# Seams and down part of an MLP laid out anew: early places, a fixed product order, four X banks, some pairs stored in two parts

## The chip, the cores and the metric

The kernel runs on one core of a Trainium2 chip. The metric is the device time of one execution, in microseconds. The profile comes from one further execution with the hardware profiler on. Engines are named as in the profile: PE (TensorE, matmuls), PEld (its weight loads), DVE (VectorE), ACT (ScalarE), POOL (GpSimd) and SP (SyncE, whose queue issues nearly all transfers).

## What is computed

One layer of a decoder trunk, in float32, for 2048 tokens of width 1024:

```python
a   = rmsnorm(x, norm_pre_mix)
mix = token_mixer(a, ...)                  # mLSTM heads and latent attention heads, then @ w_out
x   = x + rmsnorm(mix, norm_post_mix)
m   = rmsnorm(x, norm_pre_mlp)
y   = jnp.square(jax.nn.relu(m @ w_up)) @ w_down      # D_FF = 4096
x   = x + rmsnorm(y, norm_post_mlp)
```

Only the end of the token mixer (the product with w_out) and the MLP matter here.

## The kernel before

**Precision.** Each float32 factor of a product is split into a high part, which is a cast to fp32r on ACT, and a low part, which is a subtraction on DVE. A product is three matmuls: high by high, high by low, low by high. So every operand that reaches PE costs one cast and one subtraction first.

**Fewer products.** Both MLP products work on 2 x 2 blocks with seven products instead of eight (Winograd's form). The operands of the seven are the blocks themselves or sums of them, called s1 to s4 for the weights, and "T" factors for the activations. The seven results are combined through three chains of PSUM banks, X, Y and Z: products 0, 4, 5 and 6 go one after the other into one X bank, 1 and 3 into a Y bank, 2 into a Z bank (`CHAINS`). Between two products into the same bank the running sum is read out, and the next product waits for that read-out: product 3 waits for the first read-out of Y, 4 for the first of X, 5 for the second, 6 for the third.

**Output projection** (`group`, `matrix`, `transposes`). Eight groups of 256 tokens are multiplied by w_out, which lies split in SBUF. Each token tile is then normalised, the residual is added (`post`), and the result x1 is stored in DRAM (x1d). After every 512 tokens (a row block, `blk`) eight groups of four PE transposes turn x1 around (L1822) into one of two PSUM banks, ACT scales them by the gain (L1827) into one of two staging tiles `xg`, and they are stored as raw blocks in DRAM (`xd`).

**Factors of the up part.** `sums_of_rows` (L1856 on) loads four raw blocks, makes four sums on DVE (L1867) and stores these (L1870). `factor` (L1887 on) loads one of the seven factors, for each of four slices kk of 128 columns, and splits it on ACT and DVE (L1899, L1903). The tiles of factors 0 to 3 lie in a pool of their own, those of 4 to 6 in a pool that opens when the whole output projection is over (`open_b`).

**Up part** (`up`). 32 units: two halves g of the tokens by 16 pairs p of 256 hidden columns. A unit is seven products of 12 matmuls of 512 columns. `first_factors` loads its weights into two row buffers (`wr`), makes the four sums (L1959) and splits seven factors (L1989, L1992) into the 12 weight places of the ring `w`. The results are squared after a relu on ACT (L2063, L2066), summed on DVE (L2097) into the seven hidden factors and stored in DRAM (`hd`, L2111).

**Down part** (`down`, `hidden`). Eight chunks c of two pairs each, by eight units u of 256 tokens; a unit is seven products of six matmuls (L2209 to L2211). For each unit and each of the two pairs the seven hidden factors are loaded as one tile of 128 x 896 (L2179) and split (L2183, L2187). The weights of a chunk are 14 tiles out of 20 places, 8 of them in a pool `w2` that opens after the up part. The places are given out alternating between the two pairs (`2 * j + e`). Results are added to the accumulators y in SBUF, mostly on DVE (L2230), two per unit in the middle chunks by way of ACT and GpSimd (L2243, L2246). In the last chunk `finish` normalises each row tile: squares on ACT (L2279), a total on DVE (L2282), a root on GpSimd (L2285), the scaling with the gain on DVE (L2288), and the residual on GpSimd or, for tiles 11 and 15, on DVE (L2291); then the store (L2294).

**What sets the order.** All work after the first stages is declared as operations of a planner, `Plan`: engine, cost in ns, the operations that it comes after, a key, and the buffers ("rings") that it takes and frees. `Plan.run` simulates the engines: at each step it takes the operation that can start first, and among equal starts the one with the lowest key. The code is emitted in that order, and `pin` fixes the resulting order on PE, ACT, DVE and POOL. So each engine works through a list that is settled when the kernel is built, and an instruction that waits holds up everything behind it on its engine. `"X"` operations open and close pools and take no time. A pool that opens in memory or banks of a closed one waits for that one's last readers.

Of the kernel before, what the change touches and what calls it, by code (L numbers as in the profile page):

```python
# [185 lines left out]
def trunk(ctx: ExitStack, tc: tile.TileContext, x, xT, pos, wu, uqw, ukw, uvw, wout, wup, wdn, cols, rows, consts, edge, out, dbg=None):  # L186
# [38 lines left out]
    maskb = top.tile([P, P], BF16, tag="maskb", name="maskb")  # L225
    identb = top.tile([P, P], BF16, tag="identb", name="identb")
# [84 lines left out]
    def masks():  # L311
        act.copy(maskb, maskT)
        act.copy(identb, ident)
        act.copy(identr, ident)
# [794 lines left out]
    a2 = a1 = av = ar2 = pq = pS = po = trig = V = maskneg = None  # L1109
# [39 lines left out]
    def switch3():  # L1149

        nonlocal av, ar2, pS, po, V
        s_b.close()
        av = sb(pa, "av", 1, "right")
        ar2 = sb(pa, "ar2", 2, "right")
# [478 lines left out]
    for name, bufs in (("w", WB), ("wx", 4), ("wr", 2), ("xr", XR), ("st", ST), ("hr", 3), ("rb", 2), ("accA", 2), *((f"h{k}", 1) for k in range(KD))):  # L1633
        pl.ring(name, bufs)

    def wtile(name, ring="w"):

        return (pools["o1"] if ring == "wx" else pools["w2"] if ring == "w2" else pools["work"]).tile(
            [P, 2, TB], F32R, tag=ring, name=name, bufs=dict(w=WB, wx=4, w2=W2B)[ring]
        )  # L1640
# [11 lines left out]
    def right():  # L1652
        pa.close()
        pools["xa"] = sb(ctx, "xa", 1, "right")
        pools["o3"] = sb(po2, "o3", 1, "right")
        pools["pmB"] = pp(po2, "pmB", 1, "right")
        pools["ptr"] = pp(po2, "ptr", 2, "right")
# [8 lines left out]
    for name, bufs in (("accB", 1), ("ptr", 2), ("xt", 2), ("xg", 2), ("x1", XB)):  # L1666
        pl.ring(name, bufs)
# [3 lines left out]
    def matrix(k):  # L1671
        t = {}
        ring = "w" if 2 * k < WB else "wx"
# [5 lines left out]
        def hi(c):  # L1679
            wo[k, c] = wtile(f"wo{k}_{c}", ring)  # L1680
            act.copy(wo[k, c][:, 0], t["r"][:, c * TB : (c + 1) * TB])
# [6 lines left out]
        for c in range(2):  # L1688
            b = pl.op("Activation", 520, lambda c=c: hi(c), [a], key, take=(ring,))
            o_w[k, c] = pl.op("DVE", 602, lambda c=c: lo(c), [b], key, free=[("wr", a)])  # L1690
            w_free[k, c] = (ring, b)

    o_x1, x1s = {}, {}

    def group(g):
# [50 lines left out]
        for k in range(KD):  # L1746
            c, d = tile_(k)
            for t in range(GT):
# [5 lines left out]
                if k == 0:  # L1754
                    o_acc.append(prev[t])

        def post(t):
# [42 lines left out]
            pl.op("SP", 500, store, [f], key, free=[("x1", e)], kb=512)  # L1800
# [11 lines left out]
    def transposes(blk):  # L1812
        g, s = divmod(blk, 2)

        def one(k):
            q = {}
            i = (7 if s else 0) if k < 4 else (3 if s else 2)

            def tr():
                q["p"] = pools["ptr"].tile([P, 4, P], F32, tag="t", name=f"xtr{blk}_{k}")  # L1820
                for t in range(4):
                    pe.transpose(q["p"][:, t], x1s[4 * blk + t][:, k * P : (k + 1) * P], ident)  # L1822
                q["p"] = q["p"].rearrange("p t i -> p (t i)")

            def raw():
                q["x"] = pools["o3"].tile([P, TB], F32, tag="xg", name=f"xg{blk}_{k}", bufs=2)
                act.activation(q["x"], q["p"], AF.Copy, scale=pools["gcol"][:, k : k + 1])  # L1827
# [3 lines left out]

            key = END + 20 * (TB // n) * (blk + 1) + 2
            a = pl.op("PE", 4 * 110, tr, [o_x1[4 * blk + t][1] for t in range(4)], key, take=("ptr",), free=[("x1", o_x1[4 * blk + t][0]) for t in range(4)])
            b = pl.op("Activation", 571, raw, [a], key, take=("xg",), free=[("ptr", a)])
            o_xd[g, i, k % 4] = pl.op("SP", 500, store, [b], key, free=[("xg", b)], kb=256)

        for k in range(KD):
            one(k)
# [14 lines left out]

    def sums_of_rows(g, kk):

        t = {}  # L1856
        key = UP + (g - 1) * 80 + 2 * kk + 5 if g == 0 else UP + 40 + 20 * kk
# [14 lines left out]
        p = pl.op("X", 0, place, [o_xd[g, i, kk] for i in (0, 7, 3, 2)], key, take=("xr",) * 4)  # L1872
        a = {i: pl.op("SP", 500, lambda i=i: load(i), [p, o_xd[g, i, kk]], key, kb=256) for i in (0, 7, 3, 2)}
        t1 = pl.op("DVE", 602, lambda: sub(0, 7, 0), [a[0], a[7]], key)
        t3 = pl.op("DVE", 602, lambda: sub(7, 3, 7), [a[3], t1], key)
        t2 = pl.op("DVE", 602, lambda: sub(3, 3, 0), [t3], key)
        t4 = pl.op("DVE", 602, lambda: sub(2, 2, 3), [a[2], t2], key)
        for i, at, o in ((1, 0, t1), (5, 7, t3), (4, 3, t2), (6, 2, t4)):
            o_xd[g, i, kk] = pl.op("SP", 500, lambda i=i, at=at: store(i, at), [o], key, free=[("xr", p)], kb=256)
# [7 lines left out]
    def factor(g, i, kk):  # L1887
# [3 lines left out]
        pool_ = "xa" if i < 4 else "xb"  # L1891
# [14 lines left out]
        opened = o_right if i < 4 else o_open  # L1906
        last = [o_xo[0, i, kk][2]] if g else []
        a = pl.op("SP", 500, load, [o_xd[g, i, kk], opened] + (o_last_w[0, NP - 1] if g else []), key - 4, take=("xr",), kb=256)
        b = pl.op("Activation", 520, hi, [a, opened], key, take=(f"x{i}{kk}h",))
        c = pl.op("DVE", 602, lo, [b], key, take=(f"x{i}{kk}l",), free=[("xr", a)])  # L1910
# [3 lines left out]
    def open_a():  # L1914
        pA.close()
        pools["u0"] = pp(ctx, "u0", 1)

    o_openA = pl.op("X", 0, open_a, o_accA, UP)

    def open_b():  # L1920
        po1.close()
        po2.close()
        pools["u1"] = pp(ctx, "u1", 1, "right")
        pools["xb"] = sb(pX, "xb", 1, "right")
        pools["ub"] = sb(pB, "ub", 1)

    o_open = pl.op("X", 0, open_b, pl.groups["out"] + [o_openA], UP)
    for s in range(2):
        for z, bufs in (("X", 2), ("Y", 1), ("Z", 1)):
            pl.ring(f"{z}{s}", bufs, o_open if s else o_openA)  # L1930
    SLOTS = {"11": 2, "12": 1, "22": 1, "21": 1, "s1": 1, "s2": 1, "s4": 1, "p1": 1, "p5": 1, "u2": 1}
    for z, bufs in SLOTS.items():
        pl.ring(f"t{z}", bufs, o_open)
# [3 lines left out]

    def bank(s, z, name):
        return pools[f"u{s}"].tile([P, TB], F32, tag=z, name=name, bufs=2 if z == "X" else 1)

    def first_factors(nm, key, src, kind, ring, after=()):
# [22 lines left out]
        if up:  # L1964
            s1 = pl.op("DVE", 602, lambda: add("s1", (1, 0), (1, 1), add_), [a[1]], key - 10, take=("st",))
            s3 = pl.op("DVE", 602, lambda: add((1, 0), (0, 0), (1, 0), sub_), [s1, a[0]], key - 9)
            s2 = pl.op("DVE", 602, lambda: add("s2", "s1", (0, 0), sub_), [s1, a[0]], key - 9, take=("st",))
            s4 = pl.op("DVE", 602, lambda: add("s4", (0, 1), "s2", sub_), [s2], key - 8, take=("st",))
            what = [((0, 0), a[0]), ("s1", s1), ((0, 1), a[0]), ("s4", s4), ("s2", s2), ((1, 0), s3), ((1, 1), a[1])]
        else:  # L1970
            s1 = pl.op("DVE", 602, lambda: add("s1", (0, 1), (0, 0), sub_), [a[0]], key - 10, take=("st",))
            s3 = pl.op("DVE", 602, lambda: add((0, 1), (1, 1), (0, 1), sub_), [s1, a[1]], key - 9)
            s2 = pl.op("DVE", 602, lambda: add("s2", (1, 1), "s1", sub_), [s1, a[1]], key - 9, take=("st",))
            s4 = pl.op("DVE", 602, lambda: add("s4", (1, 0), "s2", sub_), [s2], key - 8, take=("st",))
# [6 lines left out]
        def one(i, w, o):  # L1981
# [12 lines left out]
            b = pl.op("Activation", 520, hi, [o], key - 8 + i, take=(ring[i],))  # L1994
            c = pl.op("DVE", 602, lo, [b], key - 8 + i, free=[("st", held[w])] if isinstance(w, str) else [("wr", p)])
# [7 lines left out]
    hd = {(p, g): dram.tile([4, P, 7, P], F32, tag=f"hd{p}_{g}", name=f"hd{p}_{g}") for p in range(NP) for g in range(2)}  # L2003
# [4 lines left out]
    def products(nm, s, i, pieces, passes, t, after, key, free, ns):  # L2008
# [4 lines left out]
        for j, piece in enumerate(pieces):  # L2013
# [6 lines left out]
            last = pl.op("PE", ns, mm, after[j] + ([last] if j else []) + after["all"], key, take=(f"{z}{s}",) if new and j == 0 else (), free=free[j])  # L2020
# [6 lines left out]
    def up(g, p):  # L2027
        nu = g * NP + p
        s = nu % 2
        key = UP + UNIT * nu  # L2030
        w = first_factors(f"u{g}_{p}", key, lambda e: wup[2 * p + e], "up", ["w"] * 7, [o_w[KD - 1, 1]])
# [4 lines left out]
        def product(i, after):  # L2036
# [12 lines left out]
            last = products(nm, s, i, [(kk,) for kk in range(4)], passes, t, af, key + 2.5 * i, fr, 660)  # L2049
# [18 lines left out]
        def both(o, after, free=()):  # L2068
            k = key + 10
            a = after if o != "21" else None  # L2070
            r = pl.op("Activation", 540, lambda: relu(o), [after], k, take=("t21",) if o == "21" else (), free=free)
            q = pl.op("Activation", 540, lambda: square(o), [r], k)
            return (r if o == "21" else a), q

        p1 = product(0, [o_openA])
        v1 = pl.op("Activation", 540, lambda: save("p1", "X"), [p1], key + 2, take=("tp1",))
        p5 = product(1, [])
        v5 = pl.op("Activation", 540, lambda: save("p5", "Y"), [p5], key + 2, take=("tp5",))
        p2 = product(2, [])
        c11 = pl.op("DVE", 640, lambda: plus("11", "Z", "p1"), [p2, v1], key + 5, take=("t11",), free=[(f"Z{s}", t_o(t, "Z", pl)), ("tp1", v1)])  # L2080
        p3 = product(3, [v5])
        p6 = product(4, [v1])
        v2 = pl.op("Activation", 540, lambda: save("u2", "X"), [p6], key + 8, take=("tu2",))
# [324 lines left out]
```

## Time and profile before

| | |
|---|---|
| median of 3 runs | 2621.9 us (2618.11 to 2624.91) |
| profiled execution | 2622.13 us |
| its span, first to last instruction | 2620.4 us |
| granted PE clock, mean | 0.982 |
| PE / DVE / ACT / POOL busy, share of the span | 95% / 72% / 50% / 32% |
| first up matmul starts at | 1277.3 us of the span |
| first down matmul starts at | 1932.96 us of the span |

A line of a timeline gives the start in the span, the duration, engine, line, operation, output and inputs, and in brackets how long the engine sat idle before it and what released it. A matmul's duration is longer than the distance to the next one's start, since matmuls are pipelined; how fast PE works is read from starts or from counts. A row of a table of stretches gives the stretch, its length, then for PE, PEld, DVE, ACT and POOL the busy time and the count of instructions, then the granted PE clock, the DMA share and GB/s. A line of a group gives count, busy time and mean duration, then the idle time before these instructions.

### The profile page before, as it was taken

To read this page: it belongs to the slowest core of one execution; us is meant where nothing else is said; L and a number is where in the kernel's file an instruction comes from. 1 tells how busy PE (TensorE), PEld (TensorE's weight loads), DVE (VectorE), ACT (ScalarE), POOL (GpSimd) and SP (SyncE) were. 2 spreads that over 40 slices of the span, in tenths; PEclk is the share of its full clock that TensorE was granted. 3 is DMA by queue.
4 is the path that set the end of the run, shared out by engine and by line. 5 is a ranking of instruction groups with operands and counts; after the bars stand their busy time and mean duration, and the time that the engine had idled before them with its cause. 6 is when DMAs were issued, how large, how long until landed. Compare 5 with 4: busy or idle time off the path is not lost. (4 is left out here: it accounts for less than half of the span.)

```text
span 2620.4 us, 33126 instructions
## 1 busy us (share of the span) xinstructions
PE 2486.6 (95%) x11107; PEld 1956.8 (75%) x11107; DVE 1895.7 (72%) x3090; ACT 1316.6 (50%) x2481; POOL 832.5 (32%) x673
## 2 busy tenths in 40 slices
PE   8999999899999999899899999999989999999997
PEld 6778787676677777687778888888867777787775
DVE  5876658699999999755676567656556677776788
ACT  5544444366666676544455556555544333433343
POOL 3442423367877787422000000000000222322235
PEclk9999999899999999999899999999989999999999
DMA  6555544400000000577886547645453333333346
GB/s 215 152 167 155 162 143 130 126 9 9 13 7 11 11 9 16 156 222 246 305 257 197 145 139 223 177 144 154 145 163 117 108 116 111 115 117 106 117 161 231
DMA packets 256179, 347.66 MB, mean 133 GB/s; under 512 B 28316, under 2 KB 169128, under 8 KB 255816
## 3 DMA queue, kind: packets, MB, share of 16 engines
q1 hardware_dynamic: 252424, 338.16, 42.3%
q0 software_dynamic: 3584, 7.39, 1.1%
q8 instruction: 87, 1.43, 0.2%
q14 instruction: 84, 0.69, 0.1%
HBM read 237.25 MB, written 108.22 MB: 132 GB/s over the span
## 5 line engine op out<-in xcount | busy, mean ns | idle before, releaser
L1467 POOL TENSOR_TENSOR pl<-p,ph 128x512 fp32r<-128x512 f32 (+1 forms) x267 | 336.2, 1273 | 144.2 <-ACT p L1463 90.7
L2246 POOL TENSOR_TENSOR y<-vd_0X,y 128x512 f32<-128x512 f32 x6 | 9.2, 1532 | 784.5 <-ACT vd_0X L2243 784.5
L1459 ACT ACTIVATE ph<-S 128x512 fp32r<-128x512 f32 (+1 forms) x320 | 170.7, 535 | 134.8 <-PE S L196 37.1
L1492 DVE SCALAR_TENSOR_TENSOR t<-ph,V,t 128x512 f32<-128x512 f32 x152 | 174.0, 1145 | 2.9
L194 PE MATMUL mm<-xh,wh 128*128 128x512 f32 x384 | 159.7, 416 | 9.5 <-ACT xh L339 7.9
L2187 DVE TENSOR_TENSOR hl<-hr,hh 128x896 fp32r<-128x896 f32 x128 | 147.0, 1154 | 18.6 <-ACT hh L2183 18.6
L196 PE MATMUL mm<-xh,wl 128*128 128x512 f32 x384 | 152.7, 398 | 0.0
L195 PE MATMUL mm<-xl,wh 128*128 128x512 f32 x384 | 152.4, 397 | 0.0
L1463 ACT ACTIVATE p<-S 128x512 f32<-128x512 f32 (+1 forms) x267 | 144.1, 541 | 9.7 <-POOL pl L1467 8.7
L1401 DVE TENSOR_REDUCE mp<-m 128x1 f32<-128x512 f32 x192 | 127.4, 681 | 21.3 <-PE m L1396 19.8
L2183 ACT CAST hh<-hr 128x896 fp32r<-128x896 f32 x128 | 115.8, 943 | 37.6 <-issue 8.5
L194 PE MATMUL S<-Qh,Kh 97*128 97x512 f32 (+1 forms) x320 | 123.0, 385 | 3.2 <-ACT p L1463 1.6
L1396 PE MATMUL m<-Kh,Qh 96*128 96x512 f32 (+2 forms) x320 | 113.0, 399 | 13.6 <-DVE mp L1401 10.3
L1479 PE MATMUL o<-pl,V 128*128 128x512 f32 (+1 forms) x320 | 121.0, 381 | 4.9 <-DVE pl L1467 2.6
L1476 PE MATMUL o<-ph,V 128*128 128x512 f32 (+1 forms) x320 | 120.5, 377 | 0.6 <-DVE ot L1547 0.5
L195 PE MATMUL S<-Ql,Kh 97*128 97x512 f32 (+1 forms) x320 | 119.5, 373 | 0.0
L196 PE MATMUL S<-Qh,Kl 97*128 97x512 f32 (+1 forms) x320 | 119.2, 372 | 0.0
L373 ACT CAST wh<-wr 128x1024 fp32r<-128x1024 f32 (+1 forms) x65 | 66.7, 1032 | 93.2 <-PE mm L195 56.4
L2063 ACT ACTIVATE t<-t 128x512 f32<-128x512 f32 x96 | 60.8, 633 | 95.5 <-DVE t L2058 94.4
L194 PE MATMUL op<-wo,hh 128*128 128x512 f32 x256 | 102.2, 399 | 2.3 <-DVE osm L1768 2.3
L195 PE MATMUL op<-wo,hh 128*128 128x512 f32 x256 | 100.7, 393 | 2.0 <-DVE wo L1684 2.0
L196 PE MATMUL op<-wo,hl 128*128 128x512 f32 x256 | 100.5, 393 | 0.0
(6388 smaller groups left out, 7658.2 us busy)
## 6 DMA issues: line engine op xcount, KB each, us to landing
hr<-hd SPq DMA_DIRECT2D x128, 448.0 KB
hd<-t SPq DMA_DIRECT2D x128, 256.0 KB
wr<-in_wu_dram SPq DMA_DIRECT2D x63, 512.0 KB
hd<-ts SPq DMA_DIRECT2D x96, 256.0 KB
xt<-in_x_dram SPq DMA_DIRECT2D x28, 512.0 KB
xf<-xd SPq DMA_DIRECT2D x56, 256.0 KB
hr<-hT SPq DMA_DIRECT2D x64, 128.0 KB
x1d<-x SPq DMA_DIRECT2D x16, 512.0 KB
```

The costliest lines, as they stand in the source:

```text
L194: pe.matmul(o, ah, bh, start=start, stop=False)
L195: pe.matmul(o, ah, bl, start=False, stop=False)
L196: pe.matmul(o, al, bh, start=False, stop=stop)
L1401: vec.tensor_reduce(mp["t"][:, j, kb : kb + 1], ps, axis=AX.X, op=ALU.max)
L1459: act.activation(t["h"][:, :w], t["S"][:, :w], AF.Exp)
L1463: act.activation(t["p"][:, :w], t["S"][:, :w], AF.Exp)
L1467: (pool if by_pool else vec).tensor_tensor(t["l"][:, :w], t["p"][:, :w], f32(t["h"][:, :w]), ALU.subtract)
L1476: pe.matmul(oo, v[:, 2:130], t["h"][:, :w], start=start, stop=False)
L1479: pe.matmul(oo, v[:, 2:130], t["l"][:, :w], start=False, stop=stop)
L1492: vec.scalar_tensor_tensor(to, hv, v0, acc["t"][:, TB - w :], ALU.mult, ALU.add)
L2183: act.copy(t["h"], t["r"])
L2187: vec.tensor_tensor(t["l"], t["r"], f32(t["h"]), ALU.subtract)
```

## The change

All of it is in the planner's declarations; the arithmetic of the products stays.

1. **Costs.** The planner's costs of the output projection and the MLP are set anew (casts 520 to 610, subtractions 602 to 690, three matmuls 660 to 695, read-outs 540 or 640 to 610 or 690).
2. **First seam.** Row blocks 2 and 3 are no longer transposed in the output projection. They are loaded again from x1d within the up part (keys from unit 3 on), four loads of 64 KB for each group of four transposes, which use the X banks and are scaled in place of the loaded tile. For the first half, factors 0, 1, 2 and 3 are split straight from the tiles of `sums_of_rows`, without the way through DRAM. The keys of the sums move earlier for the first half and later for the second.
3. **Banks and pools.** The two transpose banks become X0 and X1 of the up part; four X banks, two Y and two Z banks are separate rings. Y, Z and the working tiles `ub` open once the accumulators of the projection's first pool are read and its last matmul is done; X2 and X3 still open with `open_b`. Three slices of factor 4 move to `ub`. The slot of tile 11 goes from two buffers to one.
4. **Pairs in two parts.** Pairs 2, 6, 10 and 13 (`TWO`) are split into high and low part in the up part, through two tiles `hs`, and stored as 14 tiles; the down part loads both parts directly, with no cast and no subtraction.
5. **Down part.** Every weight place is a ring of its own. The places follow the order in which the last up units free them (`WORDER`), pair by pair (`7 * e + j`). The hidden tiles of the first two units of the first chunk take places of up factors 0, 1 and 2; all others are split in two pieces of 4 and 3 factors. The order of products on PE is written out: unit u's products 0 and 1, then 5 of the unit before, 2, 3, 6 of the unit before, 4. The last up unit's relu, squares and sums get an earlier key.
6. **Finish.** The gain is multiplied first (GpSimd; DVE for tiles 11 and 15), the scaling and the residual follow in one DVE instruction.
7. Two mask copies move from the start to the attention part (`switch3`).

```diff
-        if (g + 1) * n % TB == 0:
+        if (g + 1) * n % TB == 0 and (g + 1) * n <= HB:
             transposes((g + 1) * n // TB - 1)
...
+            if g:
+                key = UP + UNIT * (3 + 4 * s + k / 2)
+                r = pl.op("SP", 2000, load, [o_x1d[4 * blk + t] for t in range(4)] + [o_xo[0, 6, kk][1] for kk in range(4)], key - 10, take=("xr",), kb=256)
+                a = pl.op("PE", 4 * 110, tr, [r], key, take=(f"X{k % 4}",))
+                b = pl.op("Activation", 610, raw, [a], key, free=[(f"X{k % 4}", a)])
+                o_xd[g, i, k % 4] = pl.op("SP", 500, store, [b], key, free=[("xr", r)], kb=256)
+                return
...
-        for i, at, o in ((1, 0, t1), (5, 7, t3), (4, 3, t2), (6, 2, t4)):
-            o_xd[g, i, kk] = pl.op("SP", 500, lambda i=i, at=at: store(i, at), [o], key, free=[("xr", p)], kb=256)
+        def parts(i, o, n):
+
+            if g == 0:
+                at[i] = factor(g, i, kk, lambda: t[n], o, p)
+                return at[i]
+            return o
...
     def open_a():
         pA.close()
+        po1.close()
         pools["u0"] = pp(ctx, "u0", 1)
+        pools["ub"] = sb(pB, "ub", 1)
...
-    SLOTS = {"11": 2, "12": 1, "22": 1, "21": 1, "s1": 1, "s2": 1, "s4": 1, "p1": 1, "p5": 1, "u2": 1}
+    SLOTS = {"11": 1, "12": 1, "22": 1, "21": 1, "s1": 1, "s2": 1, "s4": 1, "p1": 1, "p5": 1, "u2": 1}
...
+    TWO = {p: p in (2, 6, 10, 13) for p in range(NP)}
+    hd = {(p, g): dram.tile([4, P, 14 if TWO[p] else 7, P], F32, tag=f"hd{p}_{g}", name=f"hd{p}_{g}") for p in range(NP) for g in range(2)}
...
+                b = pl.op("Activation", 610, hi, [made, *readers], k + 1, take=("hs",))
+                made = pl.op("DVE", 690, lo, [b], k + 1)
...
-        key = DN + 9.2 * (8 * c + u) + 2 * e
+        key = DN + 9.7 * (8 * c + u) + 2 * e
+        first = c == 0 and u < 2
+        parts = [(0, 4), (4, 3)]
+        if first:
+            tags = {(z, m): early[12 * u + 6 * e + 2 * n + m] for n, z in enumerate("rhl") for m in range(2)}
...
-            ring = ["w" if (14 * c + 2 * j + e) % (WB + W2B) < WB else "w2" for j in range(7)]
+            ring = [f"w{WORDER[(14 * c + 7 * e + j) % (WB + W2B)]}" for j in range(7)]
...
+    for u in range(NU + 1):
+        line += [(u, 0), (u, 1), (u - 1, 5), (u, 2), (u, 3), (u - 1, 6), (u, 4)]
+    line = [turn[x] for x in line if x in turn]
+    for a, b in zip(line, line[1:]):
+        pl.ops[b[0]][3].append(a[1])
```

More of the change, by code (lines that the diff above doesn't have):

```diff
@@ L1672, in matrix @@
         t = {}
-        ring = "w" if 2 * k < WB else "wx"
+        ring = ["wx" if 2 * k >= WB else f"w{2 * k + c}" for c in range(2)]
         def load():
@@ L2018, in mm @@
                 passes(t[z], *piece, new and j == 0, j == len(pieces) - 1)
-            last = pl.op("PE", ns, mm, after[j] + ([last] if j else []) + after["all"], key, take=(f"{z}{s}",) if new and j == 0 else (), free=free[j])
+            last = pl.op("PE", ns, mm, after[j] + ([last] if j else []) + after["all"], key, take=(bk(s, z),) if new and j == 0 else (), free=free[j])
             if new and j == 0:
@@ L2121, in trunk @@
         sums_of_rows(0, kk)
-    for i in range(7):
+    for i in range(4, 7):
         for kk in range(4):
@@ L2189, in hidden @@
-        a = pl.op("SP", 500, load, [o_dr, *o_hd[p, g]], key - 10, take=("hr2",), kb=448)
-        b = pl.op("Activation", 880, hi, [a], key - 5, take=("hh2",))
-        d = pl.op("DVE", 1003, lo, [b], key - 5, take=("hl2",), free=[("hr2", a)])
-        return t, d, [("hh2", b), ("hl2", d)]
+        key = DN + 9.7 * (8 * c + u) + 2 * e
[3 more added lines that the diff above has]
+            tags = {(z, m): early[12 * u + 6 * e + 2 * n + m] for n, z in enumerate("rhl") for m in range(2)}
+        else:
+            tags = {(z, m): f"{z}{e}{m}" for z in "hl" for m in range(2)}
@@ new lines, in new, with load @@
+        def new(z, m, dt):
+            if first:
+                t[z, m] = pools["xa"].tile([P, TB], dt, tag=tags[z, m], name=f"h{z}{m}_{c}_{u}_{e}")
+            else:
+                t[z, m] = pools["dr"].tile([P, parts[m][1] * P], dt, tag=tags[z, m], name=f"h{z}{m}_{c}_{u}_{e}", bufs=HHB)
+        def load(z, m, off):
+            j0, nj = parts[m]
+            new(z, m, F32 if z == "r" else F32R)
+            o = t[z, m][:, : nj * P]
+            dma(o if z == "r" else f32(o), hd[p, g][i][:, off + j0 : off + j0 + nj].rearrange("p j t -> p (j t)"))
@@ new lines, in loadr, with hi, lo @@
+        def loadr():
+            r = pools["dr"].tile([P, 7 * P], F32, tag="hr2", name=f"hr_{c}_{u}_{e}", bufs=HRB)
+            dma(r, hd[p, g][i].rearrange("p j t -> p (j t)"))
+            for m, (j0, nj) in enumerate(parts):
+                t["r", m] = r[:, j0 * P : (j0 + nj) * P]
+        def hi(m):
+            new("h", m, F32R)
+            w = parts[m][1] * P
+            act.copy(t["h", m][:, :w], t["r", m][:, :w])
+        def lo(m):
+            new("l", m, F32R)
+            w = parts[m][1] * P
+            vec.tensor_tensor(t["l", m][:, :w], t["r", m][:, :w], f32(t["h", m][:, :w]), ALU.subtract)
```

309 lines of the change are left out of this document (181 added, 128 removed).

## The prediction

> **What bounds the kernel now.** I read the page first, then a table of busy time by stage, then TensorE's own order of time at the three kinds of place where that table shows less work than time. The page says that TensorE is nearly always busy:
>
> ```profile
> span 2620.4 us, 33126 instructions
> ...
> PE 2486.6 (95%) x11107; PEld 1956.8 (75%) x11107; DVE 1895.7 (72%) x3090; ACT 1316.6 (50%) x2481; POOL 832.5 (32%) x673
> ```
>
> The product work is not touched by the change, so what it can gain is TensorE's lost time after the attention part. The stages: end of the output projection, its seam with the up part, the up part, its seam with the down part, seven chunks of the down part, the eighth, the tail. The x behind PE busy counts matmuls.
>
> ```profile
> core 0: us, PE busy (x) PEld busy (x) DVE busy (x) ACT busy (x) POOL busy (x), PEclk, DMA share, GB/s
> 1255.00:1277.30 22.30, 22.30 (x101) 18.31 (x100) 16.20 (x23) 11.66 (x23) 1.27 (x2) 1.00 0.94 334
> 1277.30:1304.10 26.80, 20.30 (x79) 15.23 (x78) 15.55 (x23) 13.98 (x25) 1.72 (x2) 0.75 0.77 254
> 1304.10:1915.00 610.90, 610.09 (x2618) 491.29 (x2617) 389.83 (x615) 340.87 (x600) 0.00 (x0) 1.00 0.60 178
> 1915.00:1933.00 18.00, 6.79 (x28) 4.58 (x26) 9.51 (x17) 8.67 (x14) 0.00 (x0) 0.78 0.60 191
> 1933.00:2520.00 587.00, 568.25 (x2362) 446.04 (x2363) 405.27 (x526) 222.19 (x338) 135.39 (x96) 0.99 0.37 114
> 2520.00:2610.00 90.00, 80.78 (x328) 59.70 (x326) 84.98 (x120) 35.27 (x76) 53.12 (x43) 1.00 0.69 230
> 2610.00:2620.40 10.40, 0.00 (x0) 0.00 (x0) 6.28 (x10) 1.44 (x4) 0.55 (x1) 0.73 0.50 176
> ```
>
> The up part is full: 610.9 / 2618 = 0.2333 us per 512-column matmul, my yardstick. A product of an up unit (12 matmuls) then takes 2.8 us, one of a down unit (6) 1.4 us, a down unit (7 products) 9.8 us. By this yardstick the second seam loses 18.0 - 28 x 0.2333 = 11.5 us, the seven chunks 587.0 - 2362 x 0.2333 = 35.9, the eighth 90.0 - 328 x 0.2333 = 13.5. In the first seam 32 of the 79 are short transposes:
>
> ```profile
> 1290.78 0.60 PE L1822 MATMUL xtr<-cst,x 128*128 128x128 f32 x4
> ...
> 1295.57 1.11 PE L1822 MATMUL xtr<-cst,x 128*128 128x128 f32 x4 [2.49 <-ACT xg L1827]
> ```
> ```profile
> 1294.83 0.69 ACT L1827 ACTIVATE xg<-xtr,gcol 128x512 f32<-128x512 f32 x1 [2.46 <-DMA xd<-xg]
> ```
>
> Four without a wait take 0.60 at most, say 0.45 by their starts (an estimate), so eight fours are 3.6 us, 47 products 11.0, and 26.8 - 14.6 = 12.2 us is lost. The rows tell by what: transposes of the last row block wait for ScalarE's scaling, and that for the store of a staging tile of which there are two. In all 12.2 + 11.5 + 35.9 + 13.5 = 73.1 us lost, and 10.4 of tail.
>
> **The first seam.** Blocks 2 and 3 leave the output projection. The up part opens all Y and Z banks and its working tiles once the last projection matmul is done and its pair of accumulators read, instead of (second set of banks, working tiles) after the whole post-processing; it takes its first two X banks from the earlier transposes, and gets factors 0 to 3 straight from the sums in SBUF: 16 loads and 4 stores of 256 KB fewer. So neither wait shown above is left. The 12 factor loads that remain now wait until all four sums have their staging tiles; behind them on SP stand weight loads, a unit ahead of need. New lateness can come from factors 5 and 6, whose tiles still open when all of the projection's post-processing is over; they are used 14 us into unit 0, and the planner can put products of unit 1 before them. I leave 2 us (bounds 0 and 6): 10.2 gained.
>
> The 16 fours that are moved cost 16 x 0.45 = 7 us of TensorE in the up part and free as much before it, where the row 1255 to 1277 has TensorE busy throughout: zero. Each also brings four load issues on SP, one ScalarE scaling and one store into the up part. They come due from unit 3 on, long after unit 0 frees the staging tiles, so loads lie ahead of need; were they not, TensorE's queue would stand behind each.
>
> **Pairs in two parts.** Pairs 2, 6, 10 and 13 are split after the activation: 4 pairs x 2 halves x 7 tiles = 56 casts on ScalarE, 56 subtractions on VectorE, 56 more stores. The price of each is in the rows of the same forms:
>
> ```profile
> L1899 ACT CAST x_01h<-xf x2: 603/612/621, 1155.5 to 1585.3; 128x512 fp32r<-128x512 f32 x2
> L1903 DVE TENSOR_TENSOR x_01l<-xf,x_01h x2: 683/688/693, 1156.2 to 1588.7; 128x512 fp32r<-128x512 f32 x2
> ```
> ```profile
> hd<-t SPq DMA_DIRECT2D x128, 256.0 KB
> ```
> ```profile
> L2187 DVE TENSOR_TENSOR hl<-hr,hh 128x896 fp32r<-128x896 f32 x113 | 125.0, 1109 | 14.6 <-ACT hh L2183 14.6
> ```
> ```profile
> L2183 ACT CAST hh<-hr 128x896 fp32r<-128x896 f32 x112 | 101.2, 944 | 16.3 <-issue 8.5 <-PE d_1X L2210 4.1 <-PE d_0X L2210 2.2
> ```
>
> That is 56 x 0.612 = 34 us of ScalarE and 56 x 0.688 = 39 of VectorE beside an up part in which they are busy 341 and 390 of 611: both have cover. In the down part 4 x 8 = 32 splits go, 32 x 1.109 = 35 us of VectorE and 30 of ScalarE. The other 96 are cut into pieces of 512 and 384 columns, 0.69 + 0.55 (in proportion between the two rows, an estimate) against 1.109: 96 x 0.13 = 12 us come back. VectorE nets 23 less of 490. For the denser up part I charge 2 us (bounds 0 and 10: one 1.2 us wait per two-part unit).
>
> **The second seam.** Now the first hidden tiles are loaded only when every store of the last up unit is issued:
>
> ```profile
> 1924.53 0.69 DVE L2097 TENSOR_TENSOR ts<-t,ts 128x512 f32<-128x512 f32 x1 [1.06 <-ACT t L2066]
> ```
> ```profile
> 1926.84 1.87 SPq L2179 DMA_DIRECT2D hr<-hd  x2
> ```
> ```profile
> 1931.97 1.99 ACT L2183 CAST hh<-hr 128x896 fp32r<-128x896 f32 x2 [3.75 <-DMA hr<-hd]
> ```
> ```profile
> 1932.96 0.79 PE L2209 MATMUL d_0X<-d,hh 128*128 128x512 f32 x1 [9.75 <-ACT hh L2183]
> ```
>
> From issue to use is 5.1 us, and the splits follow. The change puts the tiles of the first two down units into places of factors 0 to 2, free once product 2 of the last up unit is over, four products (11.2 us) before its end. 5.1 + 0.6 + 0.7 fits. The third unit's tiles still wait for the last store, but are due only 12 products, 16.8 us, into the down part. VectorE was idle 8.5 of the 18 us and gets 4 splits (5 us) more there, and some weights earlier. I leave 4 us (bounds 0 and 9): 7.5 gained. The slot of up tile 11, now one buffer instead of two, can be judged here: the products of a unit end at 1932.96 - 9.75 = 1923.2, its last store is issued before 1926.84, 3.6 us later (two-part pairs: 1.3 more), and the next unit writes the slot 8.4 us in. A delay would only hold a Z bank, of which there are two.
>
> **Inside the down part.** Losses sit at the changes of chunk, here from the third to the fourth:
>
> ```profile
> 2122.14 0.33 SPq L1951 DMA_DIRECT2D d7r<-in_wdn_dram  x1
> ...
> 2177.01 0.33 SPq L1951 DMA_DIRECT2D d7r<-in_wdn_dram  x1
> ```
> ```profile
> 2182.46 0.68 DVE L1959 TENSOR_TENSOR d7s<-d7r 128x512 f32<-128x512 f32 x1
> ...
> 2191.41 0.68 DVE L1992 TENSOR_TENSOR d<-d7s,d 128x512 fp32r<-128x512 f32 x1
> ```
> ```profile
> 2182.00:2201.00 19.00, 14.97 (x52) 10.66 (x53) 17.93 (x23) 9.35 (x16) 5.02 (x3) 0.91 0.34 105
> ```
> ```profile
> 2193.75 0.49 PE L2211 MATMUL d_1X<-d,hl 128*128 128x512 f32 x1 [2.20 <-DVE hl L2187]
> ...
> 2195.34 0.63 PE L2209 MATMUL d_0X<-d,hh 128*128 128x512 f32 x1
> 2195.76 0.63 PE L2210 MATMUL d_0X<-d,hh 128*128 128x512 f32 x1
> ```
>
> The second half of pair 7's weights is loaded only at 2177, since the two row buffers are held by pair 6, and all its sums and splits fall between 2182 and 2192, in the new chunk. VectorE is busy 17.93 of 19, a hidden split comes late, TensorE loses 19 - 52 x 0.2333 = 6.9 us. The cause is the old order of places: the six spare weight places go to factors 0 to 2 of both pairs, so that pair 6 keeps the rows until places free up. The new order fills them with factors 0 to 5 of the first pair. That empties the row buffers in the middle of the chunk; only 8 splits (5.5 us) and up to two sums are left for the boundary, beginning when product 0 of the last unit frees the first place, 9.8 us before need. The fixed order lays two products of 1.4 us between a read-out of the X bank and the product that waits for it, where VectorE answers in 0.69. Its price: whatever is late stops TensorE with all that is queued behind. But the old order was pinned too. I leave one product of 1.4 us for each of seven boundaries, 10 us (bounds 0 and 35.9): 25.9 gained.
>
> [...] After the 2.20 us wait above the starts are 0.42 apart instead of 0.23. [...]
>
> **The last chunk and the tail.** Here VectorE is the bound, with 84.98 of 90 us in the row above. The change swaps which half of the final step GpSimd does; the count on VectorE stays, and 16 splits in pieces add 2 us. 87 - 328 x 0.2333 = 10.5; I leave 10: 3.5 gained. In the tail, gain goes ahead of the root:
>
> ```profile
> 2614.25 0.75 DVE L2288 SCALAR_TENSOR_TENSOR y<-y,fsm,gpm 128x512 f32<-128x512 f32 x1 [0.73 <-POOL fsm L2285]
> 2615.03 0.69 DVE L2291 TENSOR_TENSOR y<-y,fx 128x512 f32<-128x512 f32 x1
> 2615.64 0.74 DVE L2288 SCALAR_TENSOR_TENSOR y<-y,fsm,gpm 128x512 f32<-128x512 f32 x1
> 2616.42 0.69 DVE L2291 TENSOR_TENSOR y<-y,fx 128x512 f32<-128x512 f32 x1
> ```
>
> Two of these four remain after the root: 1.4 us. The new planner costs and moved mask copies I take at zero.
>
> **Sum.** 10.2 - 2 + 7.5 + 25.9 + 3.5 + 1.4 = 46.5. From the span 2620.4 to 2573.9; outside the span lie 1.7 us (the profiled execution took 2622.13, 0.2 above the median 2621.9): 2575.
>
> **The rivals.** *Nearly all gaps close*: 10 us left of the 73.1 and nothing charged to the up part: 63.1 + 1.4 gained, 2558. For it: the up part has shown that this chip runs 611 us without a gap. Against: VectorE's 87 us in the last chunk. *Only the seams close*: the boundaries stay VectorE-bound, as 17.93 of 19 suggests, and the last chunk too: 10.2 + 7.5 + 1.4 - 2 = 17, so 2605. *It does not do what it says*: early tiles queue on SP behind the last stores, boundaries stay, one seam closes, and the up part gives that back: 2617. *Slower*: the DMA queues become the bound in the up part. 56 x 256 KB plus 4.2 MB for the reloaded rows are 18.9 MB; at 178 GB/s for a share of 0.60, a full share moves 297, so 64 us of transfer. Exposed in full it turns 2575 into 2639; it decides for slower once 47 us show. Against: 0.40 x 611 = 244 us are free. For: the row at 1255 stands at 0.94, and two-part unit 6 falls together with the reloads.
>
> **How the numbers follow.** The sum: 0.50, with its own range 2562 to 2590. Nearly all: 0.13. Seams only: 0.25. Not as said: 0.06. DMA: 0.06. The range goes from 2554 to 2608 and leaves out the last two and a little. This kernel's runs spread over 0.26%, so 0.3% is about what can be told from no change: faster 0.88, same 0.06, slower 0.06.
>
> **What would show it.** Right: no transposes between the last projection matmul and the up part's second unit; no idle over 2 us between last up and first down product; weight splits spread over the last unit of a chunk; matmul rate in the up part as before. Wrong: waits of TensorE for VectorE at every boundary, waits for reloaded rows or weights in the up part, a DMA share near 1 there.

## The result and the profile after

The changed kernel takes 2559.7 us (median of 4 runs, 2558.9 to 2562.91), against 2621.68 (4 runs, 2618.11 to 2624.91) for the kernel before: a ratio of 0.9766, 95% interval 0.9749 to 0.9783. The forecast was 2575, range 2554 to 2608. First the page of the changed kernel:

```profile
span 2557.2 us, 33782 instructions
...
PE 2458.0 (96%) x11107; PEld 1951.1 (76%) x11107; DVE 1911.1 (75%) x3210; ACT 1339.3 (52%) x2601; POOL 836.1 (33%) x673
```

The same 11107 matmuls, more work on DVE and ACT, and a span that is 63 us shorter. The busy time by stage, cut at about the same events as before the change (the stretch from 1268.2 is the up part, from 1895.7 down products come in, 2460 lies in the last chunk, 10.4 us after its start; the cut at 2520 before the change lay 5.0 us after it):

```profile
core 0: us, PE busy (x) PEld busy (x) DVE busy (x) ACT busy (x) POOL busy (x), PEclk, DMA share, GB/s
1245.00:1268.20 23.20, 23.20 (x103) 19.00 (x103) 18.68 (x33) 13.31 (x27) 1.38 (x2) 1.00 0.86 276
1268.20:1895.70 627.50, 627.27 (x2730) 506.78 (x2729) 442.76 (x695) 391.35 (x693) 1.41 (x2) 1.00 0.72 215
1895.70:1910.00 14.30, 14.30 (x63) 11.40 (x62) 11.69 (x21) 9.40 (x18) 0.00 (x0) 1.00 0.64 196
1910.00:2460.00 550.00, 548.23 (x2349) 440.65 (x2348) 392.30 (x581) 215.64 (x387) 140.41 (x97) 1.00 0.47 149
2460.00:2547.50 87.50, 77.85 (x304) 59.47 (x303) 76.49 (x124) 32.86 (x82) 48.16 (x42) 0.94 0.68 226
2547.50:2557.20 9.70, 0.07 (x1) 0.00 (x0) 5.17 (x9) 1.33 (x4) 0.86 (x1) 0.71 0.63 216
```

By the yardstick of 0.2333 us a matmul, the up part holds 2666 products and 64 transposes, 622 + 7 us of work in 627.5: no loss. The down part up to the last chunk needs 2349 x 0.2333 = 548.0 of 550.0. The last chunk loses 87.5 - 304 x 0.2333 = 16.6 us, more than the 13.5 before. So both seams and the chunk boundaries are closed, and the last chunk is the one place that got worse. Its two rows, before and after, each from the chunk's first matmul to the start of the last one:

```profile
2514.96:2609.60 94.64, 85.42 (x348) 63.78 (x347) 89.95 (x127) 35.90 (x77) 52.76 (x43) 1.00 0.67 222
2449.58:2547.17 97.59, 87.94 (x348) 67.91 (x347) 84.91 (x137) 36.82 (x91) 49.46 (x43) 0.95 0.66 217
```

VectorE has 5 us less to do there than before. PE is idle for 9.65 us, where it was 9.22, and is busy 2.5 us longer with as many matmuls, at a granted clock of 0.95 instead of 1.00.

The two seams in PE's order of time. From the last projection matmul to the first up product, and one of the moved groups of transposes:

```profile
1267.95 0.40 PE L196 MATMUL op<-wo,hl 128*128 128x512 f32 x1
1268.19 0.39 PE L2088 MATMUL 0_0X<-x_00h,u 128*128 128x512 f32 x1
...
1329.58 0.60 PE L1830 MATMUL xtr<-cst,xl 128*128 128x128 f32 x4
```

And from the last up unit (1_15) to the first down unit (d_0):

```profile
1895.44 0.39 PE L2090 MATMUL 1_15X<-x_43h,u 128*128 128x512 f32 x1
1895.67 0.39 PE L2320 MATMUL d_0X<-d,hh 128*128 128x512 f32 x1
...
1903.89 0.39 PE L2090 MATMUL 1_15X<-x_63h,u 128*128 128x512 f32 x1
1904.12 0.39 PE L2320 MATMUL d_0Z<-d,hh 128*128 128x512 f32 x1
```

Steps of 0.23 to 0.24 us throughout. At the second seam the hidden tiles are so early that down products stand between those of the last up unit and cover its read-outs as well.

At the boundary from the third to the fourth chunk (2134.85), the issues of the weight loads on SP's queue, and the 19 us that begin, like the stretch shown of the kernel before, 3.9 us into the chunk:

```profile
2081.79 2.14 SPq L1995 DMA_DIRECT2D d7r<-in_wdn_dram  x2
...
2137.74 0.33 SPq L1995 DMA_DIRECT2D d8r<-in_wdn_dram  x1
```
```profile
2138.70:2157.70 19.00, 19.00 (x84) 15.31 (x83) 14.91 (x24) 8.29 (x16) 5.32 (x5) 1.00 0.68 225
```

Both halves of pair 7 are issued 53 us before their chunk starts; before the change the second was issued 1.1 us before (2177.01, the chunk's start 2178.09). DVE has 4.1 us left in a stretch in which it had 1.1.

### The profile page after: what moved, and what is told of

Read it like the earlier page. It is cut to its first block, busy times and chain, and to the rows that moved or that the text cites. A ratio compares the mean times of both kernels' runs of the same rounds, so it can differ in the third digit from the quotient of the medians.

```text
span 2557.2 us, 33782 instructions
## 1 busy us (share of the span) xinstructions
PE 2458.0 (96%) x11107; PEld 1951.1 (76%) x11107; DVE 1911.1 (75%) x3210; ACT 1339.3 (52%) x2601; POOL 836.1 (33%) x673
## 4 chain that ended last, share of the span: by engine, by line
PE 74%; DVE 18%; issue 3%; DMA 2%; ACT 2%; POOL 1%; SPq 0%; DVEq 0%; POOLq 0%; ACTq 0%
DVE t L1492 4%; PE mm L194 2%; PE mm L196 2%; PE mm L195 2%; DVE mp L1401 2%; PE op L194 2%; PE op L195 2%; PE op L196 2%; PE m L1396 2%; PE o L1479 1%; PE S L194 1%; PE S L195 1%; PE o L1476 1%; PE S L196 1%; DVE m L1403 1%
## 5 line engine op out<-in xcount | busy, mean ns | idle before, releaser
L2270 ACT CAST hh<-hr 128x512 fp32r<-128x512 f32 (+1 forms) x192 | 106.7, 566 | 159.6 <-DMA hr<-hd 33.7
L2275 DVE TENSOR_TENSOR hl<-hr,hh 128x512 fp32r<-128x512 f32 (+1 forms) x192 | 128.0, 676 | 32.2 <-ACT hh L2270 23.2
L1401 DVE TENSOR_REDUCE mp<-m 128x1 f32<-128x512 f32 x192 | 127.5, 681 | 18.9 <-PE m L1396 17.3
L1396 PE MATMUL m<-Kh,Qh 96*128 96x512 f32 (+2 forms) x320 | 112.6, 398 | 14.3 <-DVE mp L1401 10.2
L195 PE MATMUL op<-wo,hh 128*128 128x512 f32 x256 | 100.2, 391 | 0.0
```

What stands on the lines that cost most here:

```text
L195: pe.matmul(o, ah, bl, start=False, stop=False)
L1396: pe.matmul(ps[:, :n], Qh[s][0:96, q0 : q0 + P], Kh[s][0:96, kb * TB : kb * TB + n], start=True, stop=True)
L1401: vec.tensor_reduce(mp["t"][:, j, kb : kb + 1], ps, axis=AX.X, op=ALU.max)
L2275: vec.tensor_tensor(t["l", m][:, :w], t["r", m][:, :w], f32(t["h", m][:, :w]), ALU.subtract)
```

## The experiments

The edits below are to the changed kernel unless "before" is named; long ones are shown in part. A chunk starts with its first `d_0X` matmul; the mean of chunks 2 to 7 is a sixth of the time from the second to the eighth start, and 336 matmuls would take 78.4 us. The eighth counts to the start of the last matmul, as does the column "from projection", which starts with the first projection matmul. The last column has PE's idle time in the eighth chunk and the granted clock there. All but the medians are read from one profile each, so differences of 2 or 3 us in them say little.

| kernel | median us | from projection | starts of chunks 2 and 8 | mean of 2 to 7 | eighth | PE idle, clock |
|---|---|---|---|---|---|---|
| before | 2621.7 | 1543.7 | 2011.74, 2514.96 | 83.9 | 94.6 | 9.2, 1.00 |
| changed | 2559.7 | 1485.2 | 1976.81, 2449.58 | 78.8 | 97.6 | 9.7, 0.95 |
| e1 free order | 2564.5 | 1486.7 | 1982.31, 2453.97 | 78.6 | 101.9 | 13.5, 0.97 |
| e2 old places | 2594.8 | 1515.5 | 1989.30, 2482.76 | 82.2 | 100.2 | 14.3, 0.98 |
| e3 no two-part pairs | 2561.3 | 1486.3 | 1978.80, 2452.95 | 79.0 | 96.3 | 9.7, 0.96 |
| e4 no early tiles | 2572.9 | 1495.5 | 1986.93, 2459.55 | 78.8 | 97.6 | 9.7, 0.95 |
| e5 old costs | 2571.0 | 1495.4 | 1982.37, 2456.14 | 79.0 | 105.8 | 17.3, 0.94 |
| e6 factors by DRAM | 2565.8 | 1490.0 | 1984.91, 2457.72 | 78.8 | 96.8 | 10.4, 0.96 |
| e6b transposes back | 2571.1 | 1495.4 | 1987.74, 2460.54 | 78.8 | 97.4 | 9.7, 0.95 |
| e7 before, new places | 2595.7 | 1519.6 | 2008.29, 2493.16 | 80.8 | 90.4 | 7.0, 1.00 |
| e7 before, new costs | 2627.5 | 1549.6 | 2018.77, 2521.35 | 83.8 | 93.9 | 9.0, 1.00 |
| e8 pairs 14, 15 | 2571.7 | 1494.7 | 2000.95, 2478.17 | 79.5 | 84.1 | 2.2, 1.00 |
| e9 pair 14 for 13 | 2558.8 | 1483.0 | 1980.41, 2454.84 | 79.1 | 88.2 | 5.2, 0.98 |
| e10 old finish | 2573.4 | 1499.5 | 1981.90, 2454.68 | 78.8 | 110.5 | 18.7, 0.91 |

**The written-out order.**

```diff
     for a, b in zip(line, line[1:]):
-        pl.ops[b[0]][3].append(a[1])
+        pass
```

> The changed kernel without the written-out order of down products: the planner chooses the order by its keys again. Theory (the order of weight places is what closed the chunk boundaries): the seven boundaries stay closed, and the time stays within 6 us of 2559.7. Rival (the fixed order closed them, by leaving two products between a read-out and the product that needs it): waits return at the boundaries and some 20 to 34 us come back, 2580 to 2594.

Ratio to before 0.9791 (0.9771 to 0.9811). The boundaries stay closed (78.6). The median is 4.8 us higher, but the two intervals overlap, and from the first projection matmul on the profiles differ by 1.6 us; the eighth chunk is 4.3 us longer. The rival falls: the order did not close the boundaries.

**The order of the weight places, taken back, and alone in the kernel before.**

```diff
-            ring = [f"w{WORDER[(14 * c + 7 * e + j) % (WB + W2B)]}" for j in range(7)]
+            ring = [f"w{WORDER[(14 * c + 2 * j + e) % (WB + W2B)]}" for j in range(7)]
```

> The changed kernel with the weight places given out alternating between the two pairs, as before the change. Theory: the second pair's rows are loaded late again and 20 to 34 us come back at the seven boundaries, 2580 to 2594, more than before the change if the fixed order lets PE do nothing else. Rival (fixed order or calibrated costs did it): within 6 us of 2559.7.

Ratio 0.9905 (0.988 to 0.993): 35 us come back, a little over the upper end of the theory. In the profiles 8 of them lie in the first chunk, 21 in chunks 2 to 7 and 3 in the eighth; 5 lie ahead of the projection, where the edit does nothing. At the boundary at 2153.96, the weight loads, PE's wait, and the stretch:

```profile
2146.44 0.33 SPq L1995 DMA_DIRECT2D d7r<-in_wdn_dram  x1
2151.35 0.34 SPq L1995 DMA_DIRECT2D d7r<-in_wdn_dram  x1
```
```profile
2156.83 0.50 PE L2321 MATMUL d_0X<-d,hh 128*128 128x512 f32 x1 [1.77 <-DVE d L2036]
```
```profile
2154.00:2173.00 19.00, 17.23 (x68) 13.47 (x67) 18.49 (x24) 8.42 (x15) 6.63 (x4) 0.91 0.58 188
```

The second half of pair 7 is again loaded just before the boundary, DVE is full (18.49 of 19), and PE waits for a weight split. The reverse test changes only the same formula in the kernel before:

```diff
-            ring = ["w" if (14 * c + 2 * j + e) % (WB + W2B) < WB else "w2" for j in range(7)]
+            ring = ["w" if (14 * c + 7 * e + j) % (WB + W2B) < WB else "w2" for j in range(7)]
```

> The kernel before with one edit: the weight places are given out pair by pair, as in the change. Theory: this alone closes most of the boundaries, 20 to 34 us less, 2588 to 2602. Rival (it needs the fixed order or the new costs): within 6 us of 2621.9.

Ratio 0.9903 (0.9878 to 0.9927): 25 us from one line (2595.65 against 2620.84 beside it). 18 us of it lie in chunks 2 to 7. Both ways the places carry the larger part of the boundaries: of the 30 us by which chunks 2 to 7 got shorter in all, the new places alone bring 18, and taking them back costs 21.

**The planner's costs.** Old costs in the changed kernel (casts 520, subtractions 602, and so on), then about the new ones in the kernel before. Of the first edit, the split of the weights:

```diff
-            b = pl.op("Activation", 610, hi, [o], key - 8 + i, take=(ring[i],))
-            c = pl.op("DVE", 690, lo, [b], key - 8 + i, free=[("st", held[w])] if isinstance(w, str) else [("wr", p)])
+            b = pl.op("Activation", 520, hi, [o], key - 8 + i, take=(ring[i],))
+            c = pl.op("DVE", 602, lo, [b], key - 8 + i, free=[("st", held[w])] if isinstance(w, str) else [("wr", p)])
```

> The changed kernel with the planner's costs of the projection and the MLP as before the change (casts 520, subtractions 602, read-outs 540 or 640, three matmuls 660), all else as changed. Theory: the costs matter little once places and order are as they are, within 8 us of 2559.7. Rival (the new costs are what makes the pinned order fit the chip): 2575 or more, with waits of PE for VectorE spread over the down part.

Ratio 0.981 (0.9783 to 0.9837), 11 us back: between the two. The waits are not spread, as the rival had it; the boundaries stay closed (79.0) and the eighth chunk takes 8 us more.

> The kernel before with one kind of edit: the planner's costs of the projection and the MLP set to about those of the change. Theory: the costs do not move the second pair's load at the chunk boundaries, so the time stays within 8 us of 2621.9. Rival (the costs are what closes the boundaries): 2595 or less.

Ratio 1.0026 (1.0016 to 1.0037): the costs alone make the old layout slower by 0.16% to 0.37%. They are worth something, 10 or 11 us, only with the new layout.

**Two-part pairs.**

```diff
-    TWO = {p: p in (2, 6, 10, 13) for p in range(NP)}
+    TWO = {p: p in () for p in range(NP)}
```

> The changed kernel with no pair stored in two parts. Theory: VectorE has cover in the middle chunks without it, so the boundaries open little: 2560 to 2570. Rival (the relief of VectorE by 23 us is what closes the boundaries of the chunks that hold a two-part pair): waits at those boundaries, 2575 or more.

Ratio 0.9772 (0.9749 to 0.9796), not to be told from the change's. The four pairs bring nothing that can be measured.

**The early hidden tiles.**

```diff
-        first = c == 0 and u < 2
+        first = False
```

> The changed kernel with the hidden tiles of the first two down units in the ordinary tiles, which open after the last up store. Theory: the second seam opens again to about the 11.5 us that it had, plus a slow stretch: 2570 to 2576. Rival (the earlier keys of the last up unit and the weights that are ready earlier closed it): 2560 to 2564.

2572.9 us, ratio 0.9826 (0.98 to 0.9852): 13 us back, as the theory said (10 in the profiles from the projection on). PE's first down product:

```profile
1909.83 0.80 PE L2320 MATMUL d_0X<-d,hh 128*128 128x512 f32 x1 [8.52 <-ACT hh L2270]
```

**The first seam.** Factors 0 to 3 by way of DRAM again, in three places:

```diff
-            if g == 0:
+            if False:
                 at[i] = factor(g, i, kk, lambda: t[n], o, p)
...
-            if i > 1 or g:
+            if True:
...
-    for i in range(4, 7):
+    for i in range(7):
```

> The changed kernel with factors 0 to 3 of the first half going by way of DRAM again (16 loads and 4 stores more), while row blocks 2 and 3 are still transposed in the up part. Theory (the transposes of the last block and their two staging tiles were the first seam's wait): the seam stays nearly closed, up to 6 us back, 2560 to 2566. Rival (the direct split is needed to have the factors in time): 10 us or more back, 2570 to 2580.

2565.83 us, ratio 0.9796 (0.9772 to 0.9821): 6 us back, the end of the theory's range. Then row blocks 2 and 3 transposed in the projection, from the tiles there instead of loads (in part):

```diff
-        if (g + 1) * n % TB == 0 and (g + 1) * n <= HB:
+        if (g + 1) * n % TB == 0:
             transposes((g + 1) * n // TB - 1)
...
-        p1 = product(0, [o_xd[0, 7, 3], o_xd[0, 3, 3]])
+        p1 = product(0, [o_xd[0, 7, 3], o_xd[0, 3, 3]] + (o_tr if nu < 2 else []))
```

> The changed kernel with row blocks 2 and 3 transposed in the projection again; the first two up units wait until all transposes are done, since they share the X banks. Theory: the first seam opens to 12 us or more, since the last block's transposes wait for its post-processing and its staging tiles: 2572 to 2582. Rival (the seam was closed by direct factors and banks): within 6 us of 2559.7.

2571.11 us, ratio 0.9815 (0.9791 to 0.984): 11 us back, just under the theory's 12. PE's waits in e6, for factors, then in e6b, for the scaling of transposes and for the projection's post-processing (L1779):

```profile
1275.73 0.50 PE L2089 MATMUL 0_0Y<-x_10l,u 128*128 128x512 f32 x1 [1.84 <-DVE x_10l L1931]
1279.39 0.50 PE L2089 MATMUL 0_0Y<-x_12l,u 128*128 128x512 f32 x1 [2.02 <-DVE x_12l L1931]
```
```profile
1258.83 0.66 PE L1830 MATMUL xtr<-cst,x 128*128 128x128 f32 x4 [0.67 <-ACT xg L1834]
1262.76 0.79 PE L194 MATMUL op<-wo,hh 128*128 128x512 f32 x1 [3.28 <-DVE x L1779]
```

So undoing either half of the change costs time. In e6b the first two up units had to be held back for the shared X banks, so it is not the old seam itself, and what this holding back costs is not shown apart.

**The last chunk.** Two-part pairs there instead of elsewhere (`TWO` = 14, 15):

> The changed kernel with pairs 14 and 15 stored in two parts instead of 2, 6, 10 and 13, so that the last chunk has no splits on VectorE (some 20 us less of its 76 busy us there). Theory: what PE loses in the last chunk, 16.6 us after the change, is VectorE's work and its order, and falls by 6 to 12 us: 2548 to 2555. Rival (the last chunk waits for SP's queue, in which stores stand ahead of the hidden loads, and two-part pairs add loads): no gain or a loss, 2558 to 2566.

The total, 2571.7 (ratio 0.9811, 0.9793 to 0.9828), is a loss, as the rival had it, and lies above its numbers, but not for its reason: the eighth chunk falls from 97.6 to 84.1 us, as the theory has it, and the loss moved to the second seam. ACT's last casts of pair 15, and PE behind them:

```profile
1931.30 0.62 ACT L2163 CAST hss<-ts 128x512 fp32r<-128x512 f32 x1 [2.14 <-DMA hd<-hs]
1931.82 0.61 ACT L2033 CAST d<-d1r 128x512 fp32r<-128x512 f32 x1
```
```profile
1932.49 0.79 PE L2320 MATMUL d_0X<-d,hh 128*128 128x512 f32 x1 [11.45 <-ACT d L2033]
```

The high parts leave through two buffers, each cast waits for an earlier one's store, and the cast of pair 1's weights for which PE waits stands behind them in ACT's list, since its place lies in the pool that opens after the up part. Pair 14 instead of 13 (`TWO` = 2, 6, 10, 14) avoids the last unit:

> The changed kernel with pair 14 in two parts instead of pair 13: half of the last chunk's splits leave VectorE, and the last up unit, pair 15, stays in one part, so its stores are not held up by the two buffers of the high parts as they were with pairs 14 and 15. Theory (VectorE's work in the last chunk costs PE there; with both pairs in two parts its loss was 3.1 us, with none 15.4 to 16.6): a loss of 8 to 11 us in the last chunk and no gap at the second seam, 2551 to 2555. Rival (pair 14 too lies so near the seam that its stores or VectorE work delay the first down products): the gain is given back, 2558 or more.

2558.8 us, ratio 0.9766 (0.9753 to 0.978): the eighth chunk takes 88.2, 9 us less, as the theory has it, but the first takes 4 us more, and the total is the rival's and cannot be told from the change's. No version was found that is measurably faster than the change.

The final step as before, on the new layout (in part):

```diff
-            b = pl.op("DVE", 750, lambda e=e: plus(e), [gs[e], o, x_], key, free=[("fsm", sq[0]), ("wr", x_)])
+            a = pl.op("DVE", 750, lambda e=e: scale(e), [o, o_dw], key, free=[("fsm", sq[0])])
+            b = pl.op("DVE" if end else "Pool", 690 if end else 1280, lambda e=e, v=end: plus(e, vec if v else pool), [a, x_], key, free=[("wr", x_)])
```

> The changed kernel with the final step as before the change: scaling with the gain on VectorE after the root, residual on GpSimd (VectorE for tiles 11 and 15). Theory: the new finish brings about 1 us at the tail and nothing in the last chunk: 2559 to 2563. Rival (GpSimd's gain, put ahead of the root, holds VectorE up and made the last chunk lose 16.6 instead of 13.7 us): 2553 to 2558.

2573.35 us, ratio 0.9825 (0.9812 to 0.9838): both the theory and the rival miss. The new finish is worth 14 us, 13 of them in the eighth chunk. DVE, GpSimd and PE around one of its waits:

```profile
2477.57 4.81 DVE L2394 SCALAR_TENSOR_TENSOR y<-y,fsm,gpm 128x512 f32<-128x512 f32 x4 [0.26 <-POOL fsm L2400]
2482.31 1.61 DVE L2275 TENSOR_TENSOR hl<-hr,hh 128x384 fp32r<-128x384 f32 x1
2483.84 0.68 DVE L2343 TENSOR_TENSOR y<-d_2X,y 128x512 f32<-128x512 f32 x1
...
2485.04 0.68 DVE L2343 TENSOR_TENSOR y<-d_2Y,y 128x512 f32<-128x512 f32 x1
```
```profile
2478.40 6.64 POOL L2403 TENSOR_TENSOR y<-y,fx 128x512 f32<-128x512 f32 x4 [0.35 <-DVE y L2394]
```
```profile
2485.77 0.80 PE L2320 MATMUL d_2Y<-d,hh 128*128 128x512 f32 x1 [3.89 <-DVE y L2343]
```

In the old finish each scaling on DVE sets off a GpSimd addition, which then runs beside the next scalings: four take 4.81 us, where 0.74 is one alone (2615.64 before the change), and a split of 384 columns takes 1.61 instead of 0.55 (2475.80 in the same run). The Y read-out stands behind them. That PE would have other work without the written-out order is argued and not shown: in the kernel before, a scaling took 1.78 us in the same way (2565.10) and no wait of PE in the eighth chunk was over 1.38, but no run has the old finish and the free order on the new layout. The stretched instructions have both inputs in SBUF, while a read-out, with one input in PSUM, takes 0.68 beside GpSimd (2483.84) as it does after it (2485.04).

In the new finish GpSimd's part comes before the root, and the longest wait of PE in the eighth chunk is 1.98 us instead of 3.89. The stretching is smaller, but not gone. In the changed kernel one scaling takes 1.77 us beside GpSimd, where two take 1.41 in the tail (2552.46):

```profile
2497.91 2.99 POOL L2394 TENSOR_TENSOR y<-y,gpm 128x512 f32<-128x512 f32 x2
```
```profile
2497.98 1.77 DVE L2403 SCALAR_TENSOR_TENSOR y<-y,fsm,fx 128x512 f32<-128x512 f32 x1
...
2501.97 0.68 DVE L2343 TENSOR_TENSOR y<-d_4Y,y 128x512 f32<-128x512 f32 x1
```
```profile
2502.70 0.50 PE L2320 MATMUL d_4Y<-d,hh 128*128 128x512 f32 x1 [1.97 <-DVE y L2343]
```

Three waits of PE in the eighth chunk (1.59, 1.97 and 1.98 us, at 2472.99, 2502.70 and 2526.87) are longer than any there before the change, and within 1.2 us of each PE runs at half clock (0.50) for 3.4 us:

```profile
2473.20:2476.60 3.40, 3.40 (x9) 2.64 (x9) 3.28 (x5) 0.62 (x1) 2.05 (x3) 0.50 0.67 208
2503.90:2507.30 3.40, 3.40 (x9) 2.63 (x9) 1.91 (x5) 1.70 (x4) 1.43 (x1) 0.50 0.96 299
2527.80:2531.20 3.40, 3.40 (x10) 2.62 (x9) 2.14 (x4) 1.24 (x3) 1.43 (x1) 0.50 1.01 311
```

## Why the prediction was right, and where its steps failed

*Direction and range* were right; 2575 lay 15 us too high, and 2559.7 lies below the 2562 to 2590 that the sum had for itself. By the yardstick the closed places gave 12.2 (first seam) + 11.5 (second seam) + 35.9 - 2.0 (chunks); with 3.1 lost in the last chunk and 0.7 gained in the tail that is 55.2 of the 63.2 us by which the spans differ. Of the other 8, some 4 lie ahead of the projection, and for some 4, in the projection and the up part, the sum had no term. So the nearness is in part luck: the closed places and the up part came 16 us better than forecast, the last chunk and the tail 7 worse, and 8 us came from elsewhere.

*First seam*, right: forecast 10.2 of 12.2, all gone; e6 and e6b show that undoing the direct factors or the moved transposes costs 6 and 11 us. The transposes ran in the up part without a wait of PE.

*Second seam*, right in mechanism: forecast 7.5 of 11.5, all gone, and e4 brings 13 back. What I had not seen is that down products would fill the last up unit. A part of the loss in the first seam was matmuls at half clock behind the waits (0.50 for 3.41 us from 1286.95 and for 10.24 from 1293.78); behind the wait of the second, the first 5.9 us of the down part ran at 0.50 (1932.96 to 1938.90). Both went with the waits.

*Chunk boundaries*, right in cause and too low in size: forecast 25.9, measured 33.9. The cause named, row buffers held by the first pair, is shown both ways for about two thirds of it (21 us back in chunks 2 to 7 in e2, 18 gained there by one line before, of 30). What brings the other ten or so is open: without the written order, the two-part pairs or the new costs, each taken back alone, the mean stays at 78.6 to 79.0. The hidden tiles in two pieces and the four X banks were not tried alone. The one product that I left at each boundary was caution without a row.

*The fixed order*: I gave it part of the boundaries; e1 shows none there, and in all no more than the 4.8 us between the medians.

*Two-part pairs*: the 23 us of VectorE's relief and the 2 us charged to the up part were both off PE's path. e3 shows no difference.

*The last chunk and the tail*, the step that failed: "the count on VectorE stays" gave 3.5 us gained, measured were 3.1 lost. It took the sum of VectorE's work for the price, and not what stands ahead of a read-out in its queue. But VectorE's work in the eighth chunk fell, from 89.95 to 84.91 us, and the chunk grew. PE's waits have nearly the old sum (9.65 us against 9.22) in fewer and longer pieces, and the growth comes with the three stretches at half clock (0.50 for 3.4 us each) behind the longest of them, for which the forecast had no term in this chunk. So the finish, set down at 1.4 us, is worth 14 on this layout (e10), and the eighth chunk still grew, from 94.6 to 97.6. e8 and e9 show that its waits go when the splits of its pairs, on VectorE and ScalarE both, go; e5, e1 and e10 each lengthen it. Which part of the change made the waits longer is open: the line that gains 25 us in the kernel before also has a short eighth chunk (90.4, at a clock of 1.00). In the tail 0.7 of 1.4 came: the last two instructions wait 1.20 us for the residual's load.

```profile
2550.58 0.68 DVE L2394 TENSOR_TENSOR y<-y,gpm 128x512 f32<-128x512 f32 x1
...
2552.46 1.41 DVE L2403 SCALAR_TENSOR_TENSOR y<-y,fsm,fx 128x512 f32<-128x512 f32 x2 [1.20 <-DMA fx<-x1d]
```

*Planner costs*, taken at zero: wrong by 10 or 11 us with the new layout, and of the other sign in the old one.

*The clock*: hardly any of the waits that I left at the boundaries came, so what they would have cost is not shown. In the last chunk waits of 1.59 to 1.98 us were followed by slow stretches, as the one of 2.20 us was before the change (0.50 for 3.41 us from 2194.90).

*Before the projection* the changed profile is 4 us ahead (first projection matmul at 1062.0 against 1065.9). In the fourteen profiles of this study that moment lies between 1060.1 and 1069.2. The moved mask copies do not explain it: the three kernels without them have 1063.9 to 1065.9, the eleven with them 1064.6 in the mean. I count it as variation.

The rivals: the DMA queues did not become the bound (share 0.72 in the up part, 0.75 while the rows are reloaded). "Nearly all gaps close", at 2558, is nearest to the outcome, and partly by luck: it left 10 us in all, while 2.0 are left at the boundaries and 16.6 in the last chunk.

## What to carry to other kernels

When an engine waits at every change of chunk, look for when its next operands' raw data were loaded, and by whom the buffer was held until then: giving out scarce places so that one operand set is finished before the next is begun can be worth more than a reordering (here about 20 us against at most 5). Price an edit to a helping engine by what stands ahead of the read-out in its queue, not by the sum of work, and ask of each wait that is left whether the clock drops behind it (here to 0.50, behind three waits of 1.59 to 1.98 us). Costs in a planner go with the layout that they plan for: here the same costs gained on one layout and lost on the other.

## What the runs showed of the hardware

In e10, VectorE instructions with both inputs in SBUF were stretched beside GpSimd additions (1.61 us at 2482.31 for a split that took 0.55 at 2475.80; four scalings in 4.81 at 2477.57, where one alone took 0.74 before the change), while a read-out with an input in PSUM kept 0.68 (2483.84). In e8, the casts that store through two buffers advanced with the stores: about 3.7 us for two tiles of 256 KB in the last up unit (casts at 1923.93, 1927.62 and 1931.30, each after a wait of 2.0 to 2.2 us for a store).

In the profiles before and after the change, the stretches at half clock (a granted clock of 0.50) last 3.41 us, or a multiple of it, but for the last of each, in which the execution ends; their starts lie whole multiples of 3.41 us apart (in the changed kernel 2473.2, 2503.9 and 2527.8: 9 and 7 times). Cut into slices of 3.41 us at these instants, the time from 1270 us on shows in these two profiles that every slice at full clock in which PE was idle for 1.83 us or more, in one wait or several, was followed by half clock, and none with less than 1.75; of the three with 1.75, all before the change, those at 1290.4 and 2106.2 were, and the one at 2607.9 was not. A wait of 1.69 us that ends at 2277.59 before the change lies across two slices, with about 0.9 us in each, and no slow stretch follows it; behind one as long in e7 with the new costs, which ends at 2285.59, matmuls start 0.41 to 0.43 us apart from 2286.77 to 2290.17.
